# The last mixture of experts: sorted by tokens behind four fixed ones, 24 of 32 experts in 32 slots on quarters of the matmul array

## The chip, the core and the metric

The program is one launch on one core of one Trainium2 chip. The metric is device time in microseconds (us) of that launch, the median of several runs. The engines are named as in the profile: PE is TensorE (matmuls), PEld its weight loads, DVE VectorE, ACT ScalarE, POOL GpSimd, SP SyncE, whose queue here issues the loads of the weights.

## The reference, cut to what matters

Three transformer blocks run in a row over 256 tokens of width 1024. The change lies in the mixture of experts that ends the third. Each token picks one of four groups and in it two of eight experts, so 512 token places are spread over 32 experts of hidden width 256:

```python
def hier_moe(u, w_grp, b_grp, w_exp, b_exp, w1, w3, w2):
    ...
    in_grp = jnp.take_along_axis(exp_logits, g_sel[:, :, None], axis=1)[:, 0]
    top_val, top_idx = lax.top_k(in_grp, TOP_K_3)
    top_w = jax.nn.softmax(top_val, axis=-1) * p_grp
    exp_w = jnp.sum(jax.nn.one_hot(top_idx, EXPERTS_PER_GROUP, dtype=jnp.float32) * top_w[..., None], axis=1)
    ...
    for gi in range(N_GROUPS):
        hid = jax.nn.silu(jnp.einsum('td,edf->tef', t, w1[gi])) * jnp.einsum('td,edf->tef', t, w3[gi])
        hid = hid * gate[:, gi, :, None].astype(hid.dtype)
        out = out + jnp.einsum('tef,efd->td', hid, w2[gi])
```

The output is this sum, added to the block's input and normalised once more. From the reference's inputs the tokens of the 32 experts can be counted: the four first have 21, 28, 23 and 14, and of the other 28 the fullest have 42, 25, 22, 21 and 21.

## The kernel before

The kernel is written out in program order for PE, ACT and DVE (`manual_schedule`), so on these three an instruction waits behind all that stand ahead of it. SP's queue takes the weight loads in an order that the framework's scheduler chooses; each load waits for its buffer to come free.

There are two mixtures. The first, in the middle of the program (functions with 1 in the name), already has the layout that the change brings to the last: its 32 experts are sorted by token count (class `Order`), the fullest get 128 slots, the next 64, and 16 of them 32 slots. A row of the profile that reads `128*32 128x512` is a matmul with 32 slots as its stationary columns; it takes a quarter of the array's columns, so that four can run beside each other; `128*64` takes half. Each f32 matmul is two rows of the profile.

The last mixture is `moe3`. The router's work (`Logits`, `Groups`, `Best`) gives a mask of which token goes to which expert; `Routes` turns it into each token's rank within its expert. All experts have 64 slots (`CAP3`). They are gathered four at a time: `gather3` writes one-hot matrices `oh` from ranks on DVE, and PE multiplies the tokens (split into two halves, `tokh` and `tokl`) with them, eight steps for the eight 128-wide parts of the width (L2938); it ends with the slots' gates (L2945) and the matrix that puts slots back to tokens (L2948, `st`). The steps of one gather are strewn over the four experts before it: three at the start of each expert.

The loop of `moe3` runs over the experts. For expert e, PE does three gather steps, turns expert e-1's product around (`turn`: L574 transposes), does half a scatter, and then `up` of expert e: 16 matmuls of 256 columns (32 rows of the profile, L2977) with the two weight tiles of w1 and w3 side by side. After every second expert, `down3` multiplies two experts with their w2 tiles (L3001, 16 rows), and `scatter3` (L3021, L3022) puts the pair's result back to tokens, where DVE adds it to the sum (L2797).

An expert's weights are three tiles of 1 MB: two for `up`, one for `down3`; 96 tiles in all. They go through a ring of buffers: 4 of the common ring, 4 of another pool, and 8 (`RING3`) that are added for this stage, 16 in all; the router's weights pass through one of them first. A load is issued when the matmuls that read the buffer's last tile are done. `overflow3` runs only if some expert has more tokens than slots.

Of the kernel before, what the change touches and what calls it, by code (L numbers as in the profile page):

```python
# [1085 lines left out]

class Routes:
# [20 lines left out]
    def rest(self, pool, gd, cap):  # L1108

        K, nc, n = self.K, self.K.nc, self.n  # L1110
        self.gd = gd
        ps = K.bank()
        for t in range(2):
            transpose_to(K, ps[:n, 128 * t:128 * t + 128], self.rank[:, t])
            transpose_to(K, ps[:n, 256 + 128 * t:384 + 128 * t], gd[:, t])
        if cap:
            self.gp = pool.tile([P, 2, n, 2], F32R, name="gp")
            nc.scalar.copy(self.gp[:, :, :, 0], gd)
            nc.vector.tensor_tensor(self.gp[:, :, :, 1], gd, self.gp[:, :, :, 0].bitcast(F32), op=ALU.subtract)
            self.check(pool, float(cap))  # L1120
        self.rankT = pool.tile([n, T], F32R, name="rankT")
        self.gateT = pool.tile([n, T], F32, name="gateT")
        nc.scalar.copy(self.rankT, ps[:n, :T])
        nc.scalar.copy(self.gateT, ps[:n, T:])

    def check(self, pool, cap):
# [52 lines left out]
class Order:  # L1179
# [3 lines left out]
    def __init__(self, K, pool, key):  # L1183
# [9 lines left out]
        self.b1 = pool.tile([P, 16, n], F32, name="b1cols")  # L1193
# [5 lines left out]

    def make(self, K, tmp, R, b1):  # L1200

# [11 lines left out]
        pos = tmp.tile([P, 1], F32, bufs=1, name="opos")  # L1213
# [3 lines left out]
        yield  # L1217

        ps = K.bank()
        nc.tensor.matmul(ps[0:1, :n], K.iota_p[:n], perm, start=True, stop=True)  # L1220
        nc.vector.tensor_copy(self.ids, ps[0:1, :n])
        yield
        bias_columns(K, b1, self.perm.bitcast(F32), self.b1)
        yield

        ps = K.bank()
# [8 lines left out]
        yield  # L1235

        cap = tmp.tile([P, 1], F32, bufs=1, name="ocap")
        more = tmp.tile([P, 1], F32, bufs=1, name="omore")
        nc.vector.tensor_scalar(cap, pos, float(WIDES), float(WIDE - NARROW), op0=ALU.is_lt, op1=ALU.mult)
        nc.vector.tensor_scalar(more, pos, 0.0, float(NARROW - WIDE), op0=ALU.is_equal, op1=ALU.mult)  # L1240
        nc.vector.tensor_tensor(cap, cap, more, op=ALU.add)
        nc.vector.tensor_scalar(more, pos, float(WIDES + NARROWS), float(NARROW - SLIM), op0=ALU.is_lt, op1=ALU.mult)
        nc.vector.scalar_tensor_tensor(cap, more, float(SLIM), cap, op0=ALU.add, op1=ALU.add)
        nc.vector.tensor_scalar(gt[:n], K.ident[:n, :n], cap[:n], None, op0=ALU.mult)
        ps = K.bank()
        nc.tensor.matmul(ps[:, :n], K.ones[:n], gt[:n], start=True, stop=True)
# [3 lines left out]
    def expert(self, place):  # L1250

        return self.nc.values_load(self.ids[0:1, place:place + 1], engines=(mybir.EngineType.SP,), min_val=0, max_val=E1 - 1)

# [133 lines left out]
def moe1(K, x, sums, wr, rp, b1, fill, A2, sh2, gt2, gpost, banks, man, then):  # L1387
    nc, tc, a = K.nc, K.tc, K.a
    with ExitStack() as cs:
# [32 lines left out]
        with tc.tile_pool(name="m2p", bufs=1) as pool:  # L1422
            order = Order(K, rt, rp[:, 1:34])
            b2 = K.cload("b_mlp2", [E1, D], rt)
# [964 lines left out]
RING3 = 8  # L2389
# [34 lines left out]
def consts4():  # L2424
    o = {}

    def rope(dim):
# [15 lines left out]
                                1).astype(np.float32)  # L2443
    q, s = np.arange(P)[:, None], np.arange(T)[None, :]
# [299 lines left out]
def moe3(K, x, r, A2, sh2, g2, wr, br, fin, ex, wide, banks, man):  # L2744
    nc, tc, a = K.nc, K.tc, K.a
    with ExitStack() as cs:
# [5 lines left out]
        halves(K, rt)  # L2752
        small = c2.enter_context(tc.tile_pool(name="q3s", bufs=1))
        with tc.tile_pool(name="q3", bufs=1) as pool:
# [15 lines left out]
            best = Best(K, small, groups.best(lg), 32, 2)  # L2770
            R = Routes(K, rt, best.mask, 32, lambda: tok.split(1))
            tok.h_of(2)
            tok.h_of(3)
        with ExitStack() as c3:
            pool = c3.enter_context(tc.tile_pool(name="m3", bufs=2))
            got = [[] for _ in range(8)]
            side = gather3(K, pool, R, tok, 0, got[0])
            next(side)
            tok.l_of(2)
            tok.l_of(3)  # L2780
# [4 lines left out]
            for m in ex:  # L2785
                m.pool = pool
# [5 lines left out]
            weave(side)  # L2792
            scat, prev, y = iter(()), None, None
# [15 lines left out]
            for e in range(33):  # L2809
# [11 lines left out]
                if e % 4 == 0:  # L2821
                    side = gather3(K, pool, R, tok, e + 4, got[e // 4 + 1]) if e < 28 else iter(())
# [9 lines left out]
                if new:  # L2832
                    new.xg = got[e // 4][0][:, :, e % 4]
# [28 lines left out]
        with K.banks(x=8):  # L2862
            overflow3(K, R, tok, x, g2, sums)
# [52 lines left out]
def gather3(K, pool, R, tok, e0, out):  # L2916
# [3 lines left out]
    ne, cap = 4, CAP3  # L2920
    oh = pool.tile([P, 2, ne, cap], F32R, tag="oh", bufs=1, name="oh")
    for t in range(2):
        nc.vector.tensor_tensor(oh[:, t], K.iota[:, :cap].rearrange("p (a n) -> p a n", a=1).broadcast_to([P, ne, cap]),
                                R.rank[:, t, e0:e0 + ne].rearrange("p (k a) -> p k a", a=1).broadcast_to([P, ne, cap]),
                                op=ALU.is_equal)
    sel = pool.tile([32, ne, 64], F32R, tag="selx", bufs=1, name="selx")
    nc.vector.tensor_copy(sel, K.sel[:32, e0:e0 + ne].rearrange("p (e a) -> p e a", a=1).broadcast_to([32, ne, 64]))
    xg = pool.tile([P, KD, ne, cap], F32, tag="lat", name="xg")
    gs = pool.tile([P, 2], F32, tag="gs", name="gs")
    st = pool.tile([P, 2, T], F32R, tag="st", name="st")  # L2930
    out.extend((xg, gs, st))
    yield
    for k in range(KD):
        ps = K.bank()[:, :ne * cap].rearrange("p (e s) -> p e s", e=ne)
        c = slice(128 * k, 128 * k + 128)
        for n, src in enumerate((tok.h, tok.l)):
            for t in range(2):
                nc.tensor.matmul(ps, src[:, t, c], oh[:, t], start=n == t == 0, stop=n == t == 1)  # L2938
# [15 lines left out]


class Expert3:
# [3 lines left out]
    def __init__(self, K, pool, w13, w2):  # L2960
        self.K, self.pool, self.w13, self.w2 = K, pool, w13, w2
        self.w = {}

    def load(self, q):
        self.w[q] = self.K.wraw(self.w13(q))

    def up(self, q):
# [15 lines left out]
    def turn(self):  # L2983
        self.ps = self.K.bank()[:, :256].rearrange("p (c n s) -> p c n s", c=2, n=2)
        for c in range(2):
            transpose_to(self.K, self.ps[:, c].rearrange("p n s -> p (n s)"), self.us[:, 128 * c:128 * c + 128])
# [136 lines left out]
```

## Time and profile before

| | us |
|---|---|
| median of 3 runs | 2191.95 (2190.87 to 2192.78) |
| the profiled execution | 2192.33 |
| its span, first to last instruction | 2190.6 |
| PE busy | 1976.1 (90%) |
| DVE busy | 956.9 (44%) |
| ACT busy | 641.0 (29%) |
| mean granted clock of PE | 0.946 |
| the last mixture's first matmul of an expert to its last `down3` | 1912.0 to 2167.1 |

The profiled execution is 0.38 us above the median, and 1.7 us of it lie outside the span. The shares of busy time are means over stages with different limits, so the argument reads the stage that changes.

### The profile page before, as it was taken

To read this page: it belongs to the slowest core of one execution; us is meant where nothing else is said; L and a number is where in the kernel's file an instruction comes from. 1 tells how busy PE (TensorE), PEld (TensorE's weight loads), DVE (VectorE), ACT (ScalarE), POOL (GpSimd) and SP (SyncE) were. 2 spreads that over 40 slices of the span, in tenths; PEclk is the share of its full clock that TensorE was granted. 3 is DMA by queue.
4 is the path that set the end of the run, shared out by engine and by line. 5 is a ranking of instruction groups with operands and counts; after the bars stand their busy time and mean duration, and the time that the engine had idled before them with its cause. 6 is when DMAs were issued, how large, how long until landed. Compare 5 with 4: busy or idle time off the path is not lost. (4 is left out here: it accounts for less than half of the span.)

```text
span 2190.6 us, 31912 instructions
## 1 busy us (share of the span) xinstructions
PE 1976.1 (90%) x12590; PEld 1241.0 (57%) x12590; DVE 956.9 (44%) x2027; ACT 641.0 (29%) x1176; POOL 134.7 (6%) x200
## 2 busy tenths in 40 slices
PE   6899979998899889988987978999889998899996
PEld 4775323333243324332426866998778998766664
DVE  3443212222222222222226997788565864423334
ACT  3553111011001101110105573544454543322221
POOL 4000000000010001000100001000200000000000
PEclk7999988999999999999997988999899999899998
DMA  7578999999999999999995523677442565689990
GB/s 295 201 259 335 376 420 419 419 419 419 419 420 420 419 419 420 419 419 419 420 412 199 198 73 135 233 268 287 163 153 105 208 217 202 262 346 403 394 385 21
DMA packets 97807, 680.09 MB, mean 310 GB/s; under 512 B 11760, under 2 KB 14064, under 8 KB 16112
## 3 DMA queue, kind: packets, MB, share of 16 engines
q1 hardware_dynamic: 94752, 671.00, 77.0%
q0 software_dynamic: 2320, 6.41, 0.9%
q8 instruction: 103, 1.69, 0.3%
q10 hardware_dynamic: 576, 0.53, 0.1%
q14 instruction: 56, 0.46, 0.1%
HBM read 675.79 MB, written 2.11 MB: 309 GB/s over the span
## 5 line engine op out<-in xcount | busy, mean ns | idle before, releaser
L1590 PE MATMUL bank<-w,xg 128*32 128x512 f32 (+2 forms) x2048 | 442.6, 616 | 52.8 <-DMA w<-w_mlp 52.1
L174 DVE TENSOR_TENSOR whl<-w,whl 128x1024 fp32r<-128x1024 f32 (+1 forms) x211 | 251.5, 1200 | 142.3 <-ACT whl L173 141.9
L1590 PEld LDWEIGHTS bank<-w,xg 128*32 128x32 f32 (+2 forms) x2048 | 125.7, 132 | 299.0 <-issue 213.1
L173 ACT CAST whl<-w 128x1024 fp32r<-128x1024 f32 (+1 forms) x219 | 221.3, 1029 | 225.2 <-PE bank L443 96.0
L1590 PE MATMUL bank<-w,a 128*32 128x512 f32 (+2 forms) x1024 | 256.8, 632 | 24.1 <-DMA w<-w_mlp 24.1
L1675 DVE TENSOR_TENSOR sg<-bank,b1cols 128x128 f32<-128x128 f32 (+2 forms) x64 | 25.1, 392 | 381.1 <-PE bank L1627 244.6
L1620 ACT COPY us<-bank 128x512 f32<-128x512 f32 x64 | 37.5, 586 | 505.1 <-PE bank L1590 505.1
L1590 PEld LDWEIGHTS bank<-w,a 128*32 128x32 f32 (+2 forms) x1024 | 66.0, 132 | 134.8 <-issue 103.3
L441 PE MATMUL bank<-hh,whl 128*128 128x256 f32 x448 | 130.5, 291 | 0.3 <-ACT whl L173 0.3
L443 PE MATMUL bank<-hh,whl 128*128 128x256 f32 x448 | 127.9, 286 | 1.8 <-DVE whl L174 1.8
L442 PE MATMUL bank<-hl,whl 128*128 128x256 f32 x448 | 128.1, 286 | 0.0
L1383 DVE TENSOR_TENSOR moe<-moe,bank 128x512 f32<-128x512 f32 x128 | 82.3, 684 | 101.8 <-PE bank L1378 92.2
L2977 PE MATMUL bank<-w,xg 128*64 128x256 f32 x1024 | 118.4, 384 | 0.0
L443 PE MATMUL bank<-xh,whl 128*128 128x256 f32 x400 | 112.8, 283 | 2.0 <-DVE whl L174 2.0
L441 PE MATMUL bank<-xh,whl 128*128 128x256 f32 x400 | 113.1, 284 | 0.8 <-ACT xh L1894 0.8
L442 PE MATMUL bank<-xl,whl 128*128 128x256 f32 x400 | 112.8, 283 | 0.0
L2797 DVE TENSOR_TENSOR moe<-moe,bank 128x512 f32<-128x512 f32 x60 | 39.8, 684 | 153.0 <-PE bank L3022 153.0
L2977 PEld LDWEIGHTS bank<-w,xg 128*64 128x64 f32 x1024 | 70.8, 137 | 37.7 <-issue 3.5
L443 PEld LDWEIGHTS bank<-hh,whl 128*128 128x128 f32 x448 | 86.5, 193 | 2.1 <-DVE whl L174 2.1
L441 PEld LDWEIGHTS bank<-hh,whl 128*128 128x128 f32 x448 | 86.6, 193 | 1.6 <-ACT whl L173 0.7
L442 PEld LDWEIGHTS bank<-hl,whl 128*128 128x128 f32 x448 | 86.5, 193 | 0.6 <-issue 0.5
L321 DVE SCALAR_TENSOR_TENSOR acc<-w,siluc,acc 128x256 f32<-128x256 f32 x154 | 78.3, 509 | 3.2
(725 smaller groups left out, 3489.5 us busy)
## 6 DMA issues: line engine op xcount, KB each, us to landing
w<-w_mlp SPq DMA_DIRECT2D x384, 1024.0 KB, 19.8
w<-w SPq DMA_DIRECT2D x96, 1024.0 KB, 7.9
w<-w_ada SPq DMA_DIRECT2D x48, 1024.0 KB, 5.0
w<-w_in SPq DMA_DIRECT2D x48, 1024.0 KB, 4.8
w<-w_ff SPq DMA_DIRECT2D x32, 1024.0 KB, 4.9
w<-w_out SPq DMA_DIRECT2D x12, 1024.0 KB, 5.2
w<-cmp_w SPq DMA_DIRECT2D x4, 1024.0 KB, 4.8
w<-w_ret_o SPq DMA_DIRECT2D x4, 1024.0 KB, 4.9
```

Of the source, the lines that this page charges most:

```text
L173: nc.scalar.copy(h, src)
L174: (eng or nc.vector).tensor_tensor(l, src, h.bitcast(F32), op=ALU.subtract)
L321: nc.vector.scalar_tensor_tensor(acc, wv[:, k], self.c[:, k:k + 1], acc, op0=ALU.mult, op1=ALU.add)
L441: nc.tensor.matmul(out, w.h[k][:, c], x.h[:, k], start=first and k == 0, stop=False)
L442: nc.tensor.matmul(out, w.h[k][:, c], x.l[:, k], start=False, stop=False)
L443: nc.tensor.matmul(out, w.l[k][:, c], x.h[:, k], start=False, stop=last and k == nk - 1)
L1383: nc.vector.tensor_add(out[:, t, c], out[:, t, c], ps[n])
L1590: self.K.nc.tensor.matmul(out[n % self.banks][r:r + cap], x[:, k], w[:, k % 2, 512 * n:512 * n + 512], start=k < m, stop=k >= KD - m)
L1620: (nc.scalar.copy, nc.vector.tensor_copy)[n](us[:, n], u[n])
L1675: nc.vector.tensor_tensor(o, ps, v.rearrange("p (c a) -> p c a", a=1).broadcast_to([P, 4, cap]), op=ALU.add)
L2797: nc.vector.tensor_add(out[:, k:k + 2], out[:, k:k + 2], ps)
L2977: nc.tensor.matmul(self.u[64 * n:64 * n + 64], self.xg[:, k], w[:, j, n], start=k == 0, stop=k == KD - 1)
```

## The change

The last mixture gets an order. Places 0 to 3 stay with experts 0 to 3, whatever their counts; behind them the other 28 experts are sorted by tokens, the fullest first. Places 0 to 7 keep 64 slots, places 8 to 31 have 32. For these, `up` puts even and odd parts of the width on quarters of the array and `turn` adds the two parts in an ordinary matmul with a folding matrix (`fold32`) in place of a transpose; `down3` does the same for its two halves. The groups of the gather are 4, 4, 8, 8 and 8 experts. `RING3` falls from 8 to 7, so 15 buffers are left. The weights of places 4 to 31 are addressed by a number that SP reads from `ids`, which is computed from the token counts. The check for overflow compares counts with each place's own slots.

```diff
+class Order3(Order):
+    def make(self, K, tmp, R):
+        nc = K.nc
+        self.positions(K, tmp)
+        yield
+        self.numbers(K)
+        yield
+        self.by_place(K, R)
+        self.gp = two_parts(K, self.pool, self.gd)
+        yield
+        cap = tmp.tile([P, 1], F32, bufs=1, name="ocap")
+        nc.vector.tensor_scalar(cap, self.pos, float(FULL3), float(CAP3 // 2), op0=ALU.is_lt, op1=ALU.mult)
+        nc.vector.tensor_scalar_add(cap, cap, float(CAP3 // 2))
+        self.caps(K, tmp, R, cap)
...
-RING3 = 8
+KNOWN3, FULL3 = 4, 8
+GROUPS3 = [(0, 4), (4, 8), (8, 16), (16, 24), (24, 32)]
+RING3 = 7
...
+            order.keep(best.mask)
             R = Routes(K, rt, best.mask, 32, lambda: tok.split(1))
+            made = order.make(K, rt, R)
+            next(made)
             tok.h_of(2)
             tok.h_of(3)
...
             next(side)
             tok.l_of(2)
+            next(made)
             tok.l_of(3)
...
             weave(side)
+            weave(made)
             scat, prev, y = iter(()), None, None
...
     def load(self, q):
-        self.w[q] = self.K.wraw(self.w13(q))
+        if callable(self.id):
+            self.id = self.id()
+        self.w[q] = self.K.wraw(self.w13(self.id, q))
...
+        m = self.parts
         for j in range(4):
             k = 4 * q + j
             for n in range(2):
-                nc.tensor.matmul(self.u[64 * n:64 * n + 64], self.xg[:, k], w[:, j, n], start=k == 0, stop=k == KD - 1)
+                r = 64 * n + self.cap * (k % m)
+                nc.tensor.matmul(self.u[r:r + self.cap], self.xg[:, k], w[:, j, n], start=k < m, stop=k >= KD - m)
...
+            if self.parts > 1:
+                K.nc.tensor.matmul(o, part, K.fold32, start=True, stop=True)
+            else:
+                transpose_to(K, o, part)
...
-                K.nc.tensor.matmul(y[n][64 * i:64 * i + 64], m.s[:, k], w[i][:, k, 512 * n:512 * n + 512],
-                                   start=k == 0, stop=k == 1)
+                apart = m.parts > 1
+                r = 64 * i + 32 * k * apart
+                K.nc.tensor.matmul(y[n][r:r + m.cap], m.s[:, k], w[i][:, k, 512 * n:512 * n + 512],
+                                   start=k == 0 or apart, stop=k == 1 or apart)
```

Three places in the engines' orders. The first is DVE at the start of the last mixture, from the tokens' ranks to the first gather's one-hot matrices (`oh`) and the second halves of the tokens (`tokl`). Before:

```order
L1104 TENSOR_SCALAR rank<-rank 128x64
L1106 COPY count<-bank 1x32
L2923 TENSOR_TENSOR oh<-iota,rank 128x256 x2
L2927 COPY selx<-sel 32x256
L1164 TENSOR_TENSOR tokl<-bank,tokh 128x512 x2
```

After, with `okey` (sort keys, which wait for four new matmuls of PE), `ogt` and `opos` (positions) and `perm` (the permutation):

```order
L1112 TENSOR_SCALAR rank<-rank 128x64
L1114 COPY count<-bank 1x32
L1234 SCALAR_TENSOR_TENSOR okey<-bank,route_p 128x33
L1236 TENSOR_SCALAR ogt<-okey 128x32
L1238 TENSOR_REDUCE opos<-ogt 128x1
L1239 TENSOR_SCALAR perm<-iota,opos 128x32
L2987 TENSOR_TENSOR oh<-iota,rank 128x256 x2
L2993 COPY selx<-sel 32x256
L1167 TENSOR_TENSOR tokl<-bank,tokh 128x512
L1245 CAST ids<-bank 1x32
L1167 TENSOR_TENSOR tokl<-bank,tokh 128x512
```

Four instructions stand ahead of the first `oh`, and the cast of the numbers between the two `tokl`.

The second is DVE a little later, between the first gather's end and the second gather's `oh`; `gp` are the gates in two parts, `topc` and `over` the overflow check. Before:

```order
L1119 TENSOR_TENSOR gp<-gates,gp 128x64
L1133 TENSOR_REDUCE topc<-count 1x1
L1134 TENSOR_SCALAR topc<-topc 1x1
L1136 CAST over<-topc 1x1
L2952 TENSOR_REDUCE gs<-bank 64x2 x2
L2953 TENSOR_SCALAR st<-bank,iota_14905 128x512
L2923 TENSOR_TENSOR oh<-iota,rank 128x256 x2
```

After, with ranks and gates by place (`byplace`), and each place's slots (`ocap`, `ocaps`, `caprow`):

```order
L3028 TENSOR_SCALAR st<-bank,iota_14906 128x512
L1258 COPY byplace<-bank 128x128
L1091 TENSOR_TENSOR gp<-byplace,gp 128x64
L1289 TENSOR_SCALAR ocap<-opos 128x1
L1290 TENSOR_SCALAR ocap<-ocap 128x1
L1265 TENSOR_SCALAR ocaps<-ident,ocap 32x32
L1268 COPY caprow<-bank 128x32
L1135 TENSOR_TENSOR count<-count,caprow 1x32
L1136 TENSOR_REDUCE topc<-count 1x1
L1137 TENSOR_SCALAR topc<-topc 1x1
L1139 CAST over<-topc 1x1
L2987 TENSOR_TENSOR oh<-iota,byplace 128x256 x2
```

The by-place step and the whole check now stand between `st` and the second gather's `oh`, which reads `byplace`.

The third is SP's queue where the last mixture's first tiles are loaded; `w` are tiles of w1 and w3, `w_3` tiles of w2, and the names in brackets are what a load waits for. Before:

```order
L141 DMA w<-w_3 128x2048 [waits DMAHW2_49,DVE_49,PE_49]
L141 DMA w<-w 128x2048 [waits DMAHW3_49,DVE_49,PE_49]
L141 DMA w<-w 128x2048 [waits DMAHW4_49,DVE_49,PE_49]
L141 DMA w<-w 128x2048 [waits DMAHW5_49,DVE_49,PE_49]
L141 DMA w<-w_3 128x2048 [waits DMAHW6_49]
L141 DMA w<-w_3 128x2048 [waits DMAHW7_49]
L141 DMA w<-w 128x2048 [waits DMAHW0_49]
L141 DMA w<-w 128x2048 [waits DMAHW1_49,PE_49]
```

After, with the read of `ids` ahead of place 4's tiles, the eleventh and twelfth of the stage:

```order
L141 DMA w<-w_3 128x2048 [waits DMAHW0_49,DVE_49,PE_49]
L141 DMA w<-w_3 128x2048 [waits DMAHW1_49,DVE_49,PE_49]
L141 DMA w<-w 128x2048 [waits DMAHW2_49,DVE_49,PE_49]
L141 DMA w<-w 128x2048 [waits DMAHW3_49,DVE_49,PE_49]
L1273 TENSOR_LOAD ids [waits DVE_49]
L1273 ISA x2
L141 ISA
L141 DMA w<-w 128x2048 [waits DMAHW4_49]
L141 ISA
L141 DMA w<-w 128x2048 [waits DMAHW5_49]
L141 DMA w<-w_3 128x2048 [waits DMAHW6_49]
L141 DMA w<-w_3 128x2048 [waits DMAHW7_49]
```

All loads behind the tenth tile now stand behind a wait for DVE's cast of `ids`.

## Rows read from the trace of the kernel before

**Rows 1.** Busy time by stretch, last mixture: stretch, length, engines, PEclk, DMA share, GB/s.

```profile
1902.00:1906.00 4.00, 1.18 (x9) 0.96 (x9) 2.67 (x9) 0.00 (x0) 0.00 (x0) 0.50 0.00 0
1914.00:1976.00 62.00, 60.38 (x440) 39.60 (x441) 18.04 (x46) 17.18 (x44) 0.00 (x0) 0.97 0.89 344
1976.00:2120.00 144.00, 144.00 (x1086) 94.09 (x1086) 47.21 (x99) 34.33 (x92) 0.00 (x0) 1.00 0.99 398
2120.00:2136.00 16.00, 15.47 (x118) 9.46 (x116) 5.39 (x12) 2.57 (x6) 0.00 (x0) 1.00 0.87 342
```

**Rows 2.** The same view, three stretches of the first mixture.

```profile
190.00:194.00 4.00, 3.24 (x42) 2.52 (x40) 2.81 (x12) 0.34 (x1) 0.53 (x2) 1.00 1.01 416
400.00:540.00 140.00, 134.57 (x633) 52.88 (x631) 34.28 (x78) 17.55 (x38) 12.14 (x18) 0.98 1.01 419
580.00:606.00 26.00, 17.66 (x118) 5.34 (x116) 5.20 (x12) 2.48 (x5) 1.28 (x4) 1.00 1.01 420
```

**Rows 3.** The page's DMA issues: count, KB each, us to landing.

```profile
w<-w_mlp SPq DMA_DIRECT2D x384, 1024.0 KB, 19.8
w<-w SPq DMA_DIRECT2D x96, 1024.0 KB, 7.9
```

**Rows 4.** Timeline of PE, last mixture: start, duration, line, operation, count.

```profile
2042.83 3.60 PE L3001 MATMUL bank<-w,s 128*64 128x512 f32 x16
2046.36 0.38 PE L3021 MATMUL bank<-st,yh 128*128 128x256 f32 x1
...
2047.42 0.40 PE L2938 MATMUL bank<-oh,tokh 128*128 128x256 f32 x2
...
2048.84 0.38 PE L574 MATMUL bank<-ident,us 128*128 128x128 f32 x2
2049.15 3.67 PE L2977 MATMUL bank<-w,xg 128*64 128x256 f32 x32
```

**Rows 5.** Timeline of PE, first mixture: halves, folding matmuls, quarters.

```profile
567.06 3.65 PE L1590 MATMUL bank<-w,xg 128*64 128x512 f32 x16
...
588.83 1.10 PE L1627 MATMUL bank<-route_p,us 128*128 128x64 f32 x8
...
648.90 1.92 PE L1590 MATMUL bank<-w,xg 128*32 128x512 f32 x16
```

**Rows 6.** Timeline of DVE, last mixture's start.

```profile
1903.43 0.17 DVE L1106 COPY count<-bank 1x32 f32<-1x32 f32 x1
1903.55 0.76 DVE L2923 TENSOR_TENSOR oh<-iota,rank 128x256 fp32r<-128x256 f32 x2
```

**Rows 7.** Timeline of PE and DVE, the first mixture's start.

```profile
191.89 0.63 PE L1206 MATMUL bank<-mask,ones 128*128 128x32 f32 x4
...
192.36 0.17 DVE L1106 COPY count<-bank 1x32 f32<-1x32 f32 x1
...
192.98 0.19 DVE L1210 SCALAR_TENSOR_TENSOR okey<-bank,route_p 128x33 f32<-128x33 f32 x1 [0.45 <-PE bank L1208]
...
193.86 0.41 DVE L1325 TENSOR_SCALAR oh<-iota,rank 128x64 fp32r<-128x64 f32 x2
```

**Rows 8.** Timeline of PE, last mixture: from the first gather to the second.

```profile
1915.45 0.39 PE L2948 MATMUL bank<-rankT,selx 32*128 32x256 f32 x1
...
1916.08 0.38 PE L2948 MATMUL bank<-rankT,selx 32*128 32x256 f32 x1
...
1917.69 0.92 PE L2938 MATMUL bank<-oh,tokh 128*128 128x256 f32 x2 [1.23 <-DVE oh L2923]
```

**Rows 9.** Timeline of PE and DVE, first mixture: the by-place step and the check.

```profile
219.04 0.40 PE L1230 MATMUL bank<-perm,rankT 32*128 32x32 f32 x2
...
220.69 0.29 DVE L1233 COPY byplace<-bank 128x128 f32<-128x128 f32 x1 [1.73 <-PE bank L1232]
...
221.97 0.13 DVE L1136 CAST over<-topc 1x1 int32<-1x1 f32 x1
```

**Rows 10.** Timeline of PE, last mixture: the up matmuls of the ninth expert.

```profile
1975.86 3.67 PE L2977 MATMUL bank<-w,xg 128*64 128x256 f32 x32
```

**Rows 11.** Timeline of PE, last mixture: the last down matmuls.

```profile
2163.48 3.65 PE L3001 MATMUL bank<-w,s 128*64 128x512 f32 x14 [0.42 <-DVE s L2992]
```

More of the change, by code (lines that the diff above doesn't have):

```diff
@@ L1116, in rest @@
         if cap:
[L1117 to L1120, printed above, removed]
+            self.gp = two_parts(K, pool, gd)
         self.rankT = pool.tile([n, T], F32R, name="rankT")
@@ L1212, in make, with numbers, by_place @@
         nc.vector.tensor_scalar(gt, k[:, :n], k[:, n:n + 1], None, op0=ALU.is_gt)
-        pos = tmp.tile([P, 1], F32, bufs=1, name="opos")
+        pos = self.pos = tmp.tile([P, 1], F32, bufs=1, name="opos")
         nc.vector.reduce_sum(pos, gt, axis=AX.X)
         nc.vector.tensor_scalar(self.perm, K.iota[:, :n], pos, None, op0=ALU.is_equal)
-        perm = self.perm[:n].bitcast(F32)
[L1217 to L1224, printed above, removed]
+    def numbers(self, K):
+        ps = K.bank()
+        K.nc.tensor.matmul(ps[0:1, :E1], K.iota_p[:E1], self.perm[:E1].bitcast(F32), start=True, stop=True)
+        K.nc.vector.tensor_copy(self.ids, ps[0:1, :E1])
+    def by_place(self, K, R):
+        nc, n = K.nc, E1
+        perm = self.perm[:n].bitcast(F32)
         ps = K.bank()
@@ L1234, in make, with caps @@
         nc.scalar.copy(self.rankT, ps[:n, 256:512])
[L1235 to L1244, printed above, removed]
+    def caps(self, K, tmp, R, cap):
+        nc, n = K.nc, E1
+        each = tmp.tile([P, n], F32, bufs=1, name="ocaps")
+        nc.vector.tensor_scalar(each[:n], K.ident[:n, :n], cap[:n], None, op0=ALU.mult)
         ps = K.bank()
-        nc.tensor.matmul(ps[:, :n], K.ones[:n], gt[:n], start=True, stop=True)
+        nc.tensor.matmul(ps[:, :n], K.ones[:n], each[:n], start=True, stop=True)
         nc.vector.tensor_copy(self.cap, ps[:, :n])
@@ L1423, in moe1 @@
             order = Order(K, rt, rp[:, 1:34])
+            order.b1 = rt.tile([P, 16, E1], F32, name="b1cols")
             b2 = K.cload("b_mlp2", [E1, D], rt)
@@ L2443, in consts4 @@
                                 1).astype(np.float32)
+    i = np.arange(32)
+    p = np.zeros((P, 97), np.float32)
+    p[:, :32] = 31 - i + np.where(i < KNOWN3, (KNOWN3 - i) << 16, 0)
+    p[:, 32] = np.tile(p[0, :32], 4)
+    p[:, 33:97] = np.kron(np.eye(2), np.tile(np.eye(32), (2, 1)))
+    o["route3_p"] = p
     q, s = np.arange(P)[:, None], np.arange(T)[None, :]
@@ L2752, in moe3 @@
         halves(K, rt)
+        rp = K.cload("route3_p", [P, 97], rt)
+        K.fold32 = rp[:, 33:97]
+        order = Order3(K, rt, rp[:, :33])
         small = c2.enter_context(tc.tile_pool(name="q3s", bufs=1))
@@ L2784, in moe3 @@
                 next(side)
-            for m in ex:
-                m.pool = pool
+            for p, m in enumerate(ex):
+                m.place(pool, order, p)
             ex[0].xg = got[0][0][:, :, 0]
@@ L2937, in gather3 @@
             for t in range(2):
-                nc.tensor.matmul(ps, src[:, t, c], oh[:, t], start=n == t == 0, stop=n == t == 1)
+                nc.tensor.matmul(ps, src[:, t, c], oh[:, t, :, 0], start=n == t == 0, stop=n == t == 1)
         nc.scalar.copy(xg[:, k], ps)
@@ L3044, in overflow3 @@
             with tc.For_i(0, 32) as e:
-                for base in range(CAP3, T, CAP3):
-                    pk = PickAt(K, pool, R, ctr, base)
+                for base in range(0, T - CAP3 // 2, CAP3):
+                    pk = PickAt(K, pool, R, ctr, base, cap)
                     got = []
```

134 lines of the change are left out of this document (90 added, 44 removed).

## The prediction

> **What bounds the kernel now.** I read the busy time by stretch first, since the shares over the whole span mix stages. In the last mixture, from the ninth expert on, PE is busy 144.00 of 144 us at a granted clock of 1.00 (2.4 GHz) [rows 1]: no matmul waits for anything. The loads look busy too (DMA share 0.99, 398 GB/s), but PE paces them: a load is issued only when a buffer comes free. What they do when nothing holds them back is shown by the first mixture: 419 GB/s over 140 us with PE at 134.57 of 140, and 420 GB/s where PE is busy for only 17.66 of 26 us [rows 2]. The page's issues say the same: a load takes 19.8 us to land there, in a deep queue, and 7.9 us here [rows 3]. So PE is the bound here, and the loads stand only 5% behind it (398 of 419). Any saving of PE's work is therefore cut off where the loads become the bound. That point decides the number.
>
> **What PE's work falls by.** Per pair of experts now: two times up at 3.67, down 3.60, two turns at 0.31, two half scatters at 1.06, four gather steps at 0.47 (1.42 for three; a gather has eight, for two pairs): 7.34 + 3.60 + 0.62 + 2.12 + 1.90 = 15.6 us [rows 4]. The whole way from the ninth up, 1975.86 [rows 10], to the end of the last down, 2167.13 [rows 11], is 191.3 us, or 15.9 a pair; the rest of 0.3 to 0.4 is the end of each gather. Places 8 to 31 are 12 pairs and change so:
> - up: 16 rows on quarters took 1.92 [rows 5]. The 32 rows of 256 columns of one expert carry as many columns as 16 rows of 512, whose two prices, 3.67 and 3.65, agree on halves [rows 4, 5]. So 1.92 instead of 3.67, twice a pair: −3.50.
> - down: the same rows, 1.92 instead of 3.60: −1.68.
> - turn: a folding matmul costs 1.10 / 4 = 0.275 [rows 5], two of them 0.55 against 0.31 for two transposes [rows 4]: +0.24 an expert, +0.48 a pair.
> - gather: the same eight steps now serve eight experts, two a pair instead of four: −0.95. The slots' matrix at the gather's end is made for each pair as before (a matmul of 0.38 to 0.39 [rows 8], with the gates' small ones about 0.45 by the rest above).
>
> A new pair is 3.84 + 1.92 + 1.10 + 2.12 + 0.95 + 0.45 = 10.4 us. Over 12 pairs PE is freed of 12 × 5.5 = 66 us.
>
> **What the loads allow.** A pair is six tiles, 6.29 MB; at 419 GB/s [rows 2] that is 15.0 us. It is less than PE needs now (15.9) and more than PE will need (10.4). From place 8 on the loads bound, and of PE's gain only 15.9 − 15.0 a pair can be seen, plus what PE now computes behind the last landing, since it no longer has a full ring to work off. I therefore count bytes instead of matmuls:
> - 96 tiles of 1.0486 MB. Before the first up at about 1912 the ring is full and nothing moves (DMA share 0.00 from 1902 to 1906 [rows 1]). With 15 buffers instead of 16, 81 tiles are left, 84.9 MB.
> - Places 0 to 7 are done as now, PE-paced, up to 1976 (the ninth expert's up starts at 1975.86 [rows 10]). Until then 344 GB/s × 62 us = 21.3 MB move [rows 1]. Left: 63.6 MB.
> - 63.6 MB at 419 GB/s: 151.8 us.
> - The start is later by 6.2 us (below): 1976 + 6.2 + 151.8 = 2134.0 for the last landing.
> - The last tile is one of w2. Behind it stands one down on quarters, 1.9 us: 2135.9. Now the last down ends at 2163.48 + 3.65 = 2167.1 [rows 11]. The path is 31.2 us shorter. From there to the end of the span the code is the same (23.5 us); I leave it.
>
> PE does not wait from place 8 at once: it eats a lead of 12 to 15 tiles with 6/10.4 = 0.577 tiles a us against 0.400 landing, so the first waits come some 70 to 85 us later, about 2050 to 2070.
>
> **What the start costs.** Two chains of small steps are added, both ahead of matmuls that PE waits for.
> - Ranks to the first `oh`. Now `oh` starts 0.12 us behind `count` [rows 6]; in the first mixture, with the same four steps between, 1.50 (192.36 to 193.86 [rows 7]): +1.4. The key's four matmuls end at about 192.5 to 193.0 there at a granted clock of 1.00 [rows 2, 7]; here the clock is 0.50 (1.2 GHz) at that place [rows 1], so I add 1.0. Sum 2.4; bounds 1.4 and 4, if nothing or everything of it is drawn out.
> - Second gather. It now waits 1.23 us for `oh` [rows 8]. Its `oh` comes to stand behind the by-place step and the check, which DVE does in order. In the first mixture that goes from 219.04 (first matmul) to 222.10 (end of the check, 221.97 + 0.13), 3.07 us [rows 9]. Two steps for the parts of the gates and the slots of a place are not in that stretch; at DVE's small prices (0.13 to 0.29 [rows 9]) plus their handover I take 1.6. With 0.3 up to the first by-place matmul and 0.47 for `oh` until PE can start: 5.4 from 1916.08, against 1.61 now (1916.08 to 1917.69 [rows 8]): +3.8; bounds 2 and 5.5.
>
> Together 6.2, range 4 to 9. It costs in full: no load can use the time, since every buffer that could be free is waited for by PE's next tiles. The other queue to look at is SP's: 10 tiles can be issued before the numbers are read, the rest stand behind the cast of `ids`, which comes at about 1907 (behind the first `oh` at 1903.55 + 2.4 [rows 6] and one `tokl`). Ten tiles last PE to place 3, beyond 1930, and the queue is idle then anyway. I cost it at nothing; the cover is those ten tiles, and the read would have to come some 15 us late before it showed. The reads of a register ahead of each later load cost nothing either: the first mixture has them and moves 419 GB/s [rows 2].
>
> **Sum.** The profiled execution is 2192.33, 0.38 above the median. 2192.33 − 31.2 = 2161.1. Forecast **2161 us**, 1.4% less. It moves by 1 us for each us of the start, and by 4 for each 1% of the load rate.
>
> The Trainium skill ("DMA: Bandwidth & Descriptors", section "Where 436 GB/s comes from") gives HBM's share of one core as about 358 GB/s. By it the 63.6 MB would take 178 us and the kernel about 2187. The trace does not agree: 419 GB/s over 140 us [rows 2], and that measurement decides.
>
> **The rivals.**
> 1. *The loads stay at 398 GB/s.* For: this is the rate in this stage with a DMA share of 0.99 [rows 1], as if full. Against: 7.9 us to landing is no deep queue [rows 3]. 63.6 / 0.398 = 159.8 us: +8, 2169.
> 2. *The loads fall to some 344 GB/s when 15 buffers of three pools and addresses from a register feed them.* For: 344 and 342 are seen at the two ends of the stage [rows 1]. Against: both are stretches in which PE or the end of the list sets the pace. 184.9 us: +33, 2194, no change. The change would then not show what it does.
> 3. *The loads don't bind.* Then PE's saving comes out in full: 2192.3 − 66 + 6 = 2132. Against: 63.6 MB between 1982 and 2107 would be 509 GB/s, and no stretch shows more than 420 [rows 2].
> 4. *Slower: the clock.* The mechanism is at place 8: matmuls on quarters with waits between them could hold PE at 1.2 GHz, and the pair of 10.4 us becomes 10.4/c. 12 pairs must fit into 2167 − 1982 = 185 us for no loss: it decides at a mean granted clock of 0.67. At 0.50 the pairs take 250 us: 2232 + 23.5 + 1.7, about 2257. If it fell only with the first waits, about 4.5 pairs were drawn out from 15 to 20.8 us: +26, 2187. Against: in the first mixture PE is on quarters and halves and busy for 17.66 of 26 us, 0.68, at clock 1.00 [rows 2]; 10.4 of 15.0 is 0.69.
>
> Beside the fourth stands the Trainium skill ("TensorE: Matmul & The Clock Gate", section "HAM oscillation — how this bites in real kernels"): DMA waits between bursts of matmuls send the array back to half its clock. By that rule 2187 to 2257. So far the rows at 0.68 busy do not agree.
>
> **How the numbers follow.** Forecast 0.76, first rival 0.12, second 0.03, third 0.03, fourth 0.05 (0.02 of it the milder form, which is still faster), something not on the list 0.01. About 0.2%, 4.4 us, is what a measurement of this kernel can tell from no change. Faster: 0.76 + 0.12 + 0.03 + 0.02 = 0.93; same: 0.03; slower: 0.04. The range: below, a start that costs 4 and no loss at the last tile, less a few us if the eight static places feed more than 21.3 MB: 2154. Above, the first rival with a start of 9: 2172, and 1 more for the end at a lower clock: 2173. It leaves out the rest of the rivals and a tenth of the forecast.
>
> **What would show it.** The first up at about 1914.4, the second gather's first step at about 1924, waiting for `oh` behind `byplace` and `over`; the ninth expert's up at about 1982. From there 419 GB/s, landing times towards 19 us instead of 7.9, no wait of PE until about 2050, then waits of up for `w` at a clock of 1.00; the last landing near 2134, one down of 1.9 us right behind it, and 23.5 us to the end. The quarter rows should show 1.92 for up and down, and 0.55 for a turn. The forecast is wrong if the rate from 1982 on is under 405 GB/s, if the clock in the waits falls below 0.9, if the ninth up starts later than 1985, or if PE still has work for many tiles behind the last landing. Should PE be idle before 2040, the pair or the lead was counted wrong.

## The result and the profile after

| | before | after |
|---|---|---|
| median | 2192.05 us | 2168.93 us (2167.83 to 2170.32) |
| ratio to before | | 0.9891, 95% interval 0.9878 to 0.9903 |
| the profiled execution | 2192.33 | 2170.32 |
| its span | 2190.6 | 2168.6 |
| first matmul of the ranks (L1094, after L1102) | 1901.24 | 1902.67 |
| from there to the second gather / place 8 | 16.45 / 74.62 | 22.01 / 85.51 |
| from there to the end of the last down / of the span | 265.9 / 289.4 | 241.7 / 265.9 |

The kernel is 23.1 us faster by the medians; 31.2 were forecast. The executions differ by some us in what lies ahead of the last mixture, where nothing was changed, so from here on events of the stage are counted from the ranks' first matmul. By that the stage is 289.4 − 265.9 = 23.4 us shorter.

Busy time of the kernel after by stretch (columns as in [rows 1], which it answers):

```profile
1914.00:1976.00 62.00, 58.46 (x417) 37.70 (x416) 16.00 (x48) 16.39 (x47) 0.00 (x0) 0.92 0.91 361
1976.00:1988.00 12.00, 9.70 (x67) 6.95 (x65) 6.18 (x14) 2.84 (x7) 0.00 (x0) 0.86 0.83 322
1988.00:2000.00 12.00, 12.00 (x119) 7.42 (x118) 4.10 (x8) 3.58 (x10) 0.00 (x0) 1.00 0.97 362
2000.00:2138.00 138.00, 114.86 (x1198) 67.73 (x1200) 51.13 (x101) 28.81 (x75) 0.00 (x0) 0.94 1.01 420
2138.00:2142.00 4.00, 3.06 (x22) 1.59 (x14) 1.77 (x5) 0.59 (x2) 0.00 (x0) 1.00 0.49 205
```

Before, PE was busy 144.00 of 144 us and the loads moved 398 GB/s [rows 1]. Now PE is busy 114.86 of 138 and the loads move 420, the rate of the first mixture [rows 2]. That is the forecast's change of bound. New are the second and third line, between 1976 and 2000, where the loads move only 322 and 362 GB/s, and the last line, where they fade over 4 us.

What PE waited for in the stage (line, releaser: us in total, times, longest), and the DMA issues of the last part (count, KB each, us to landing):

```profile
PE bank L3096 <- DMA w<-w: 10.5, 8, 1.5
PE bank L3022 <- DVE selx L2993: 6.9, 3, 2.3
PE bank L3076 <- ACT us L3068: 4.9, 9, 0.5
PE bank L3064 <- DMA w<-w: 2.7, 5, 0.8
```

```profile
w<-w SPq DMA_DIRECT2D x14, 1024.0 KB, 19.8
```

A load behind 2090 takes 19.8 us to land, as in the deep queue of [rows 3]; over the whole stage it was 7.9 before. The third line is a wait that the prediction's sum does not have: the folding matmuls of a `turn` (L3076) wait for ACT, 4.9 us in all. Before, such waits were 1.6 us in all.

The start, timelines of DVE and PE (they answer [rows 6, 8]):

```profile
1904.86 0.17 DVE L1114 COPY count<-bank 1x32 f32<-1x32 f32 x1
...
1907.17 0.75 DVE L2987 TENSOR_TENSOR oh<-iota,rank 128x256 fp32r<-128x256 f32 x2
...
1924.15 0.14 DVE L1139 CAST over<-topc 1x1 int32<-1x1 f32 x1
1924.22 0.74 DVE L2987 TENSOR_TENSOR oh<-iota,byplace 128x256 fp32r<-128x256 f32 x2
```

```profile
1924.68 0.91 PE L3007 MATMUL bank<-oh,tokh 128*128 128x256 f32 x2 [1.39 <-DVE oh L2987]
```

`oh` stands 2.31 us behind `count` (0.12 before), and the second gather's right behind the overflow check.

The loads at the start:

```profile
1904.00:1926.00 22.00, 15.41 (x90) 12.46 (x91) 8.94 (x39) 4.75 (x17) 0.00 (x0) 0.66 0.70 285
```

This is where SP's wait for `ids` shows. DVE's cast comes at 1908.65, nothing moves between 1904 and 1909, and then 6.3 MB come up to 1926, some six tiles. So the ring was not full when PE reached the first up: the tiles behind the tenth were still to come.

The end of the third gather, the first of eight experts, on PE and then on DVE:

```profile
1977.01 0.49 PE L3022 MATMUL bank<-rankP,selx 32*128 32x256 f32 x2
1979.81 0.46 PE L3022 MATMUL bank<-rankP,selx 32*128 32x256 f32 x2 [2.30 <-DVE selx L2993]
1980.20 0.44 PE L574 MATMUL bank<-ident,us 128*128 128x128 f32 x2
1980.57 5.36 PE L3064 MATMUL bank<-w,xg 128*64 128x256 f32 x32
...
1988.18 1.93 PE L3064 MATMUL bank<-w,xg 128*32 128x256 f32 x32
```

```profile
1977.06 1.40 DVE L3109 SCALAR_TENSOR_TENSOR yl<-bank,gs,yh 128x512 fp32r<-128x512 f32 x2
1978.38 0.33 DVE L3027 TENSOR_REDUCE gs<-bank 64x4 f32<-64x8 f32 x2
1978.72 0.75 DVE L3028 TENSOR_SCALAR st<-bank,iota 128x512 fp32r<-128x512 f32 x1
1979.39 0.27 DVE L2993 CAST selx<-sel 32x256 fp32r<-32x256 f32 x1
```

A gather of eight needs two `selx` through one buffer. The second stands on DVE behind `yl`, `gs` and `st`; PE waits 2.30 us for it. Right behind, the up of place 7 takes 5.36 us instead of the 3.67 of [rows 10], at a mean granted clock of 0.64 between 1980 and 1984. Place 8 (quarters, 1.93) starts at 1988.18.

The last waits for weights, on PE:

```profile
2137.35 1.07 PE L3064 MATMUL bank<-w,xg 128*32 128x256 f32 x16 [0.42 <-DMA w<-w]
...
2142.41 1.92 PE L3096 MATMUL bank<-w,s 128*32 128x512 f32 x14 [0.81 <-SPq L3129]
```

The profile puts the last wait down to a branch on SP; but the loads still move 41 GB/s between 2141 and 2142 and nothing after, so I read it as a wait for the last tile. PE has no such wait in e1 and e3 below, where it waits for no tile. One down of 1.92 follows, to 2144.33 (2167.13 before, [rows 11]).

### The profile page after: what moved, and what is told of

It reads as the page before. It is cut to its first block, busy times and chain, and to the rows that moved or that the text cites. A ratio compares the mean times of both kernels' runs of the same rounds, so it can differ in the third digit from the quotient of the medians.

```text
span 2168.6 us, 32093 instructions
## 1 busy us (share of the span) xinstructions
PE 1931.9 (89%) x12564; PEld 1205.2 (56%) x12564; DVE 956.3 (44%) x2027; ACT 632.3 (29%) x1154; POOL 135.6 (6%) x203
## 5 line engine op out<-in xcount | busy, mean ns | idle before, releaser
L1630 PEld LDWEIGHTS bank<-w,xg 128*32 128x32 f32 (+2 forms) x2048 | 126.3, 133 | 295.2 <-issue 216.3
L1422 DVE TENSOR_TENSOR moe<-moe,bank 128x512 f32<-128x512 f32 x128 | 82.2, 684 | 98.6 <-PE bank L1417 89.2
L3064 PE MATMUL bank<-w,xg 128*32 128x256 f32 (+1 forms) x1024 | 83.7, 406 | 2.7 <-DMA w<-w 2.7
L443 PEld LDWEIGHTS bank<-xh,whl 128*128 128x128 f32 x400 | 76.9, 192 | 2.5 <-DVE whl L174 2.5
## 6 DMA issues: line engine op xcount, KB each, us to landing
w<-w_mlp SPq DMA_DIRECT2D x384, 1024.0 KB, 19.8
```

What stands on the lines that cost most here:

```text
L443: nc.tensor.matmul(out, w.l[k][:, c], x.h[:, k], start=False, stop=last and k == nk - 1)
L1422: nc.vector.tensor_add(out[:, t, c], out[:, t, c], ps[n])
L1630: self.K.nc.tensor.matmul(out[n % self.banks][r:r + cap], x[:, k], w[:, k % 2, 512 * n:512 * n + 512], start=k < m, stop=k >= KD - m)
L3064: nc.tensor.matmul(self.u[r:r + self.cap], self.xg[:, k], w[:, j, n], start=k < m, stop=k >= KD - m)
```

## The experiments

Theory 1, the prediction's: behind place 8 the loads bind, so PE's saving shows only up to them, and the start's delay counts in full. The rivals: PE's own path decides, or the new way of loading (numbers, 15 buffers) does. In the table the last three columns are counted from the ranks' first matmul, in the profiled execution: the start of place 8's up, the end of the last down, and the end of the span, which I call the stage. The kernel after is there twice; 265.4 is the mean of its two stages. Every stage comes from one trace. Those of the kernel after and of the two that came out like it (e2, e5) lie between 264.9 and 265.9, so a difference of 1 us tells nothing. Each ratio is to the kernel before as it ran beside that kernel (medians 2192.05 to 2196.70).

| kernel | median us | ratio to before, 95% | place 8 | last down ends | end |
|---|---|---|---|---|---|
| before | 2192.05 | 1 | 74.6 | 265.9 | 289.4 |
| after | 2168.93 | 0.9891 (0.9878 to 0.9903) | 85.5 | 241.7 | 265.9 |
| after_again | 2168.77 | 0.9883 (0.9856 to 0.9910) | 85.0 | 241.0 | 264.9 |
| e1_order_only | 2197.47 | 1.0017 (1.0001 to 1.0034) | – | 270.0 | 295.2 |
| e2_static | 2168.52 | 0.9875 (0.9849 to 0.9901) | 85.0 | 241.7 | 265.6 |
| e3_half_loads | 2149.10 | 0.9787 (0.9744 to 0.9831) | 85.2 | 220.8 | 244.8 |
| e4_sixteen | 2171.04 | 0.9892 (0.9864 to 0.9921) | (149.1: place 16) | 244.5 | 268.5 |
| e5_selx | 2169.83 | 0.9878 (0.9857 to 0.9899) | 85.0 | 241.5 | 265.4 |
| e6_ring6 | 2170.70 | 0.9882 (0.9860 to 0.9904) | 85.5 | 244.1 | 268.1 |
| e7_early | 2167.47 | 0.9858 (0.9834 to 0.9883) | 82.2 | 240.1 | 264.0 |
| e8_slim_first | 2162.85 | 0.9839 (0.9815 to 0.9862) | 77.2 | 235.9 | 260.0 |
| e9_fours | 2165.47 | 0.9877 (0.9840 to 0.9913) | 79.9 | 238.3 | 263.5 |
| e10_fours_early | 2167.80 | 0.9888 (0.9855 to 0.9922) | 77.0 | 234.8 | 260.1 |
| e11_fours_early_slim | 2165.72 | 0.9879 (0.9847 to 0.9911) | 72.0 | 236.1 | 261.6 |

### The order alone

```diff
-KNOWN3, FULL3 = 4, 8
-GROUPS3 = [(0, 4), (4, 8), (8, 16), (16, 24), (24, 32)]
+KNOWN3, FULL3 = 4, 32
+GROUPS3 = [(i, i + 4) for i in range(0, 32, 4)]
```

> Kernel after, but all 32 places keep 64 slots and halves of the array, gathered four at a time as before; the sorting, the numbers read by SP, and 15 buffers stay. It prices the order alone. Theory 1 (the loads bind only behind place 8, where PE is fast; the order costs its chains at the start in full): PE is the bound throughout, as in the kernel before, and the time is that of before plus what the chains delay the second gather, 5.6 us without the drift ahead of the stage: about 2198. Rival (loads addressed from a register are slower, or 15 buffers are too few): PE waits for w in up and down, and the time is over 2204.

Measured: 2197.47, and 5.9 us more than before in the stage (the ratio gives 3.7, with an interval of 0.2 to 7.5). PE waits for no tile at all; between 1990 and 2120 it is never idle:

```profile
1990.00:2120.00 130.00, 130.00 (x992) 85.31 (x992) 44.14 (x92) 31.84 (x86) 0.00 (x0) 1.00 1.00 401
```

So the order costs its chains at the start, 5.9 us, and numbers from a register and 15 buffers cost a PE-bound kernel nothing that shows.

### Addresses known at build time

```diff
-            self.id = lambda: order.expert(p)
+            self.id = None
```

> Kernel after, but the tiles of place p are those of expert p, addressed at build time; SP reads no number. (So the sorted tokens meet the wrong experts' weights; the instructions of PE, ACT and DVE are the same.) Theory 1 (the reads of numbers cost nothing): 2169, within 1.5 us of the kernel after, although all buffers are full before the first up. Rival (the wait of SP for the numbers, or addressing from registers, holds the loads): 2160 to 2165, with the last landing earlier by as much.

Measured: 265.6 against 265.4. SP's reads cost nothing that shows, as costed. They do move loads, though. The same stretch here and in the kernel after (361 GB/s, above):

```profile
1914.00:1976.00 62.00, 58.46 (x421) 38.64 (x421) 15.86 (x47) 17.09 (x48) 0.00 (x0) 0.93 0.75 291
```

Here the ring is full early, and from the ranks' first matmul on some 85 MB are loaded, 81 tiles; in the kernel after some 90 MB, 86 tiles. The five tiles that wait for `ids` come while the loads would otherwise stand still (4 GB/s between 1903.7 and 1920 here), and so the end is the same.

### Fewer loads

```diff
+        if q and self.parts > 1:
+            self.w[q] = self.w[0]
```

> Kernel after, but places 8 to 31 use their first tile of w1 and w3 for both halves of up, so 24 of 96 tiles are not loaded (left out of the computation: the second half of these weights). Theory 1 (loads bind): a pair needs 4.19 MB, 10.0 us at 420 GB/s, and PE with 10.4 us and its waits becomes the bound: place 8 at 1988 + 12 x 10.6 + some 6 us of waits for selx = 2121 at the last down instead of 2144, about 2146. Rival (PE's path decides already, the loads only look busy): 2169 within 2 us.

Measured: 20.6 us less in the stage (244.8); the two runs took 2143.67 and 2154.53. PE waits for no `w` any more, and the loads have slack:

```profile
2000.00:2100.00 100.00, 91.18 (x995) 58.89 (x998) 42.46 (x85) 25.50 (x68) 0.00 (x0) 0.93 0.89 349
```

Compare 420 in the kernel after. This shows that the loads bind there, and that some 20 us of PE's saving lie behind them unused. With no load to hold it, PE needs (220.8 − 85.2) / 12 = 11.3 us a pair, where the prediction has 10.4.

### Sixteen places on quarters instead of 24

```diff
-KNOWN3, FULL3 = 4, 8
-GROUPS3 = [(0, 4), (4, 8), (8, 16), (16, 24), (24, 32)]
+KNOWN3, FULL3 = 4, 16
+GROUPS3 = [(0, 4), (4, 8), (8, 12), (12, 16), (16, 24), (24, 32)]
```

> Kernel after, but only places 16 to 31 have 32 slots; places 8 to 15 keep 64, gathered four at a time. PE gets 8 x 2.6 = 21 us more work. Theory 1 (the loads bind): this work is hidden except where PE paces the loads at 398 instead of 420 GB/s for four pairs, 4 x 0.9 us: 2167 to 2173. Rival (PE's work decides): 2190.

Measured: 3.1 us more in the stage (2171.04; ratio 0.9892 against 0.9891). The 21 us of PE's work are the prediction's prices; its busy time rose by 16 us (218.5 against 202.5, from 12 us behind the ranks' first matmul to 4.4 us behind the last down). The loads bind again from place 16 on:

```profile
2060.00:2140.00 80.00, 69.37 (x756) 41.51 (x755) 31.07 (x61) 17.88 (x46) 0.00 (x0) 0.96 1.01 419
```

Theory 1 stands a third time: eight of the 24 slim places bring 3 us.

### The second selx earlier

```diff
+        if q0 + 2 < pairs:
+            sel = rows_of(e0 + 2 * q0 + 4)
         if q0 == 0:
             for u in range(2):
...
-        if q0:
-            sel = rows_of(e0 + 2 * q0)
+        if q0:
+            yield
+            yield
+            yield
```

> Kernel after, but in a gather of eight the second selx is written ahead of the slots' sums and st, and the matmuls that read it come an expert's work later, so that PE need not wait for DVE there. Theory 1 (from about 2000 on the loads bind; ahead of that PE's lateness at the start holds the loads): only the first of the three waits counts, 2.3 us and some 1.7 us of the half clock behind it; the loads get back part of the 2.8 us that they lose between 1976 and 1988: 2166 to 2167. Rival A (all three waits and the half clock behind each lie on the path): 2157. Rival B (none counts): 2169.

Measured: no change in the stage, 265.4 (rival B). Place 7's up took 3.67 us again, but the wait had not gone. PE stood behind that up instead, for the next thing that DVE owed it:

```profile
1977.30 0.50 PE L3024 MATMUL bank<-rankP,selx 32*128 32x256 f32 x2
1979.33 0.36 PE L3007 MATMUL bank<-oh,tokh 128*128 128x256 f32 x1 [1.53 <-DVE oh L2987]
```

`oh` for eight experts stands behind `yl`, `gs` and `st` on DVE, and PE waits 1.53 us for it; between 1980 and 1982 the granted clock is 0.50, the lower level. Place 8 came no earlier (85.0).

### A shorter ring

```diff
-RING3 = 7
+RING3 = 6
```

> Kernel after with 14 buffers instead of 15. Theory 1: a tile fewer is loaded when PE begins, and it is added behind: 1.0486 MB at 420 GB/s, +2.5 us: 2171.4. Rival (a shorter ring also stalls PE or the loads all along): over 2176. Other rival (the ring has no say): 2169.

Measured: 2.7 us more in the stage (268.1 against 265.4). A buffer less, and so a tile less in the ring when the loads first stand still, is a tile more at the end. The medians and ratios (2170.70 and 0.9882 against 2168.93 and 0.9891) can't tell, since drift ahead of the stage blurs them.

### Ranks by place earlier

The heart of the edit (the helpers that it calls, their places in the loop and the edit of e5 are left out here):

```diff
...
         self.positions(K, tmp)
+        R.rank_rows(tmp)
         yield
         self.numbers(K)
+        ps = self.rank_by_place(K, R)
         yield
-        self.by_place(K, R)
+        self.rank_in(K, ps)
+        yield
+        self.gate_by_place(K, R)
...
```

> The edit of the second selx, and besides the ranks are turned and put by place while PE waits for the tokens' second halves, the gates by place and the overflow check come behind the second gather's oh. Theory 1: the second gather starts 4.4 us earlier, near where it did before but for the first chain, and all of it counts until the loads bind; with the 2 to 3 us of the second selx 2161 to 2163. Rival (the loads had slack at the start, so only the end of the PE-paced part counts): 2166.

Measured: the second gather starts at 19.1 instead of 22.0 to 22.8 and place 8 at 82.2, but the end gains only 1.4 us, where 6 to 8 were expected; the rival's 2166 was nearer. 3 us at the start became 1.4 at the end. At the first gather of eight (78 to 96 us behind the ranks) the loads again dipped:

```profile
1992.29:1998.29 6.00, 6.00 (x48) 2.88 (x41) 0.68 (x2) 0.69 (x2) 0.00 (x0) 1.00 0.71 270
```

So theory 1 had a hole: the stretch around that gather.

### Slim places first

The edit of e7, and besides (the gather's and the overflow check's slots for these places are left out here):

```diff
...
-        if p >= FULL3:
+        if p < KNOWN3 or p >= FULL3:
             self.cap, self.parts = CAP3 // 2, 2
```

> The kernel with early ranks, and besides places 0 to 3 have 32 slots too (they hold 28 tokens at most; more would go to the overflow branch), so only places 4 to 7 are PE-paced. Theory 1: PE frees buffers 10 us earlier ahead of place 8, and the loads, which in the kernel after have moved 6.2 MB less by 2000 than 420 GB/s from 1909 on would give (14.8 us), recover most of that: 2153 to 2158. Rival (the loads' deficit comes from the full ring before the first up alone): no faster than the kernel with early ranks.

Measured: 2162.85; 5.4 us less in the stage than the kernel after, where 11 to 16 were expected, and 4.0 less than e7, where the rival said none. Its ratio, 0.9839, is the lowest of the kernels that leave nothing out, but its interval (0.9815 to 0.9862) just meets that of after_again (0.9856 to 0.9910).

### Fours throughout, and the kernel after again

Theory 2, formed here: the boundary to the first gather of eight makes place 8 late and holds back the buffers.

```diff
-GROUPS3 = [(0, 4), (4, 8), (8, 16), (16, 24), (24, 32)]
+GROUPS3 = [(i, i + 4) for i in range(0, 32, 4)]
...
-    cap = 4 * CAP3 // ne
+    cap = CAP3 if e0 < FULL3 else CAP3 // 2
...
```

> The kernel after itself, beside the three others on one chip: 2169, and 265.9 us from the first matmul of the ranks to the end, whatever the drift ahead of the stage.

> Kernel after, but the 24 places with 32 slots are gathered four at a time, as the first eight places are. PE gets 12 x 0.95 = 11 us of gather steps more; the slots' second selx and the oh of 512 columns go. Theory 2 (what made the last landing late is the boundary to the first gather of eight, where DVE's queue makes PE wait for selx or, with that mended, for oh, and PE falls to half clock, so that buffers come free late): place 8 begins at 81 to 82 us behind the ranks instead of 85.5, and the end is 3 to 4 us earlier, 262 to 263 us behind the ranks; the 11 us of PE are hidden. Rival A (the boundary has no say, the loads bind through it): 266 within 0.5. Rival B (the steps count): 270 or more.

Measured: the kernel after gave 264.9 and 2168.77. With fours place 8 begins at 79.9, 5.3 us earlier than its mean, and the last down ends 3.1 us earlier (238.3 against 241.3; after, after_again, e2 and e5 lie between 241.0 and 241.7). Theory 2 said 3 to 4 us for the end. The added gather steps are hidden, for the loads move at their full rate:

```profile
1980.00:2120.00 140.00, 127.22 (x1319) 82.61 (x1316) 54.25 (x115) 35.57 (x104) 0.00 (x0) 0.95 1.01 419
```

The end gains only 1.9 us, because the tail behind the last down is 1.2 us longer. PE's last matmul and DVE's wait for it, first e9, then after:

```profile
2151.74 1.19 PE L530 MATMUL bank<-ident,rstd 128*128 128x128 f32 x4 [3.87 <-DVEq L3129]
2152.97 3.22 DVE L2927 SCALAR_TENSOR_TENSOR moe<-xT,g,bank 128x256 f32<-128x256 f32 x8 [4.60 <-PE bank L530]
```

```profile
2160.46 1.19 PE L530 MATMUL bank<-ident,rstd 128*128 128x128 f32 x4 [2.48 <-PEq L3129]
2162.01 3.22 DVE L2927 SCALAR_TENSOR_TENSOR moe<-xT,g,bank 128x256 f32<-128x256 f32 x8 [3.54 <-PE bank L530]
```

The profile puts L530's wait down to the branch of the overflow check (L3129) in both. But PE's own branch is not longer with fours (3.64 us against 3.75), so the cause of the longer wait stays open; e10 and e11 have the same long tail (25.3 and 25.5 us). By the medians (2165.47, runs between 2159.72 and 2171.31) the gain of fours can't be told from none.

### Fours and early ranks, and slim places first besides

The edits of e7 and e9 together (e10), and of e8, too (e11).

> Fours, and the ranks by place ahead of the second gather. Theory 2: the second gather starts some 3 us earlier and, with no boundary that gives it back, this reaches the end: 259 to 260 us behind the ranks. Rival (the loads bind ahead of it): as with fours alone.

Measured: 260.1 (expected 259 to 260), the last down 6.5 us earlier than after's mean. With the boundary gone, the 3 us of the early ranks do reach the end (260.1 against 263.5 of e9), which e7 could not show.

> The same, and places 0 to 3 in 32 slots as well. Theory 2: only the ring that is full ahead of the first up, and PE's half clock there, still hold the loads; place 8 ten us earlier, 254 to 257 us behind the ranks. Rival: as its form with gathers of eight, 260.

Measured: 261.6, not 254 to 257. Place 8 is another 5 us earlier, and the end is not. From the ranks to the second expert PE stays at half clock, and the loads stand low behind it:

```profile
1902.00:1930.00 28.00, 25.48 (x134) 20.00 (x137) 9.22 (x42) 8.03 (x26) 0.00 (x0) 0.50 0.67 262
```

```profile
1924.81:1930.81 6.00, 6.00 (x48) 4.40 (x44) 0.26 (x3) 3.00 (x6) 0.00 (x0) 0.55 0.53 175
1930.81:1936.81 6.00, 6.00 (x84) 3.69 (x76) 0.44 (x2) 2.32 (x7) 0.00 (x0) 1.00 0.78 298
1936.81:1942.81 6.00, 6.00 (x68) 4.37 (x61) 3.47 (x9) 2.49 (x7) 0.00 (x0) 1.00 0.98 397
```

The three lines of the second view are 2.3 MB short of 420 GB/s, 5.6 us. Behind them the loads move 414 to 426 GB/s in every stretch up to 2074, so what is left to win is ahead of 1943: a full ring and a slow PE. e8 starts in the same way (123 and 168 GB/s between 24 and 32 us behind the ranks). No run took that stretch away to see the end move.

## Why the prediction was right, and where its size was off

The direction and the change of bound were right, and the time lies in the range, 7.8 us above the forecast. Point by point:

- **PE's prices.** Quarters took 1.93 and 1.92 (1.92 said), two folding matmuls 0.56, or 0.66 behind a wait for ACT (0.55). Right one by one; the whole pair was 11.3 us in e3 instead of 10.4, for the sum had neither the waits for ACT's `us` (4.9 us in the stage) nor those for the later `selx`. It cost nothing here, as both are under the 15.0 us of the loads.
- **The loads bind, at 419 GB/s.** 420 over 138 us. Right, and shown by e3 and e4. The Trainium skill ("DMA: Bandwidth & Descriptors", section "Where 436 GB/s comes from") has some 358 GB/s for a core's share of HBM; the trace does not agree here either. The first rival (398 GB/s) did not come; e1 shows that 398 to 401 is PE's pace. That its 2169 is the measured time is chance: the time alone would have spoken for a mechanism that the rate rules out.
- **The start, 6.2 us.** 22.01 − 16.45 = 5.6 at the second gather, 6.3 at place 6 (65.4 against 59.1 us behind the ranks), and 5.9 for the whole order in e1. Right; of its first term (2.4) `count` to `oh` showed 2.2.
- **The numbers on SP, nothing.** Right (e2), but the byte count beside it was not: 81 tiles were said to be left at the first up, and 86 were loaded from the ranks on, since five wait for `ids`. By 1983.6, the 1982.2 of the prediction with 1.4 us of drift, 26.3 MB had moved instead of 21.3, and so 64.1 MB were left against 63.6. The same five tiles are missing on both sides, which is why the time does not show it.
- **"Places 0 to 7 are done as now"** is the step that failed. Place 8 was to be 6.2 us later and was 10.9 later (85.51 − 74.62), 4.6 of it behind place 6. The part on the gather counted steps saved; it did not look at what the first gather of eight brings ahead of the ups of places 7 and 8: a second `selx` in the same buffer and a wider `oh`, both in DVE's order behind `yl`. That is 2.30 us of waiting and 5.36 − 3.67 = 1.7 us by the lower clock. With it the loads lost ground, most of it between 1983.6 and 2000 (335 GB/s): at 2000 there were 420 × 138 + 205 × 4 = 58.8 MB left, where the prediction's line (63.6 MB at 1982.2, with the 1.4 us of drift) has 56.7. The 2.0 MB are 4.9 us.
- **The last tile** does not end at full rate: 0.82 MB took 4 us (2138 to 2142), 2.0 us more than at 420 GB/s. Behind it stood one down of 1.92, as said.
- **The tail** was 24.3 instead of 23.5 us: 0.8, 0.7 of it in DVE's last wait (3.54, 2.80 before).

4.9 + 2.0 + 0.8 = 7.7, and the forecast's 31.2 less the 23.4 of the stage is 7.8. Of the 4.9, e9 shows 3.1 to be the boundary's: without it place 8 is 5.3 and the last down 3.1 us earlier. The other 1.8 are open.

- **The clock**, the fourth rival, came in short stretches only. Behind PE's waits for `selx` it fell (5.36 for an up of 3.67; that part is in the 4.9), and at 2117 to 2121 between waits for tiles, too; but from 2000 on the loads bind, and the mean is 0.94. "TensorE: Matmul & The Clock Gate" in the Trainium skill, section "HAM oscillation — how this bites in real kernels", describes such drops behind waits on DMA; the trace shows one, from 2117 on, while the other waits for `w`, up to 1.5 us, left the clock at 1.00.
- **First waits for `w`** were said for 2050 to 2070 and came at 2085: PE began later, at 1988, and with the 11.3 us a pair of e3 it uses 0.531 tiles a us instead of 0.577, so a lead of 12 to 15 tiles lasts 92 to 115 us (an estimate from these rows), to 2080 to 2103.
- **Its own signs of being wrong** came in part: the ninth up was later than 1985 (1988.2, or 1986.8 without the drift), and the clock behind waits fell below 0.9 (0.62 between 2118 and 2122). The first is the step that failed, the second cost little. The rate stayed above 405 from 2000 to 2138, but not between 1982 and 2000.

## What to carry to other kernels

When a change frees the engine that binds, look up what the next resource does when nothing holds it, and count its bytes: the saving ends there, and here a third of the slim places is worth only 3 us (e4: 16 us more of PE's busy time cost 3 us). Then walk through the place where the old regime hands over to the new one, instruction by instruction on each engine; a stall there, ahead of the point where the loads bind, is paid for the most part (e9: place 8 5.3 us earlier, the last down 3.1), and the same stall behind it was free here (the two later waits for `selx`, with the loads at 419 to 425 GB/s around them). Taking one instruction out of a busy queue only shows the next one in it (e5).

## What the runs showed of the hardware

- Time ahead of the stage drifts: the ranks' first matmul came between 1896.0 (e9) and 1908.3 us (e7) in the profiled executions, and DVE's first add of the first mixture already between 247.2 and 257.1. So 10 of the 12 us arise early; the cause was not looked for. Effects of 2 us showed in stage times, not in medians of four runs.
- The granted clock fell to its lower level behind a wait of PE of 2.3 us, and up took 5.36 instead of 3.67; with matmuls on quarters from the first place on (e11) the granted clock stayed at 0.50 for 28 us although PE was busy for 25.48 of them.
- The loads' rate is not flat to the end: in the kernel after the last 0.82 MB came at 205 GB/s, and in after_again, e8, e9 and e10 it fades in the same way over the last 3 to 6 us.
